# Products of turned probabilities and values issued for two key tiles at a time, with two more buffers for the turned tiles

## The chip, the cores and the metric

The kernel runs on one core of a Trainium2 chip. The metric is the device time of one execution in microseconds (us), lower is better.

## What is computed

The program is one forward pass of a small network on 1024 tokens of 1024 channels, in float32: a state-space layer, a layer with forgetting attention, then a block with a windowed attention over latents and 256 context tokens and a mixture of experts, and a block with a low-rank dense attention and a mixture of experts. What matters here are its three attentions. Cut to the essentials:

```python
# forgetting attention: 16 heads of 64, 1024 queries, causal
s = einsum('bhqd,bhkd->bhqk', qi, kt) + fqi[..., None] - fk[:, :, None, :]
p = softmax(where(kpos <= qpos, s, -inf)); o = einsum('bhqk,bhkd->bhqd', p, vt)
# windowed attention: 8 heads of 64 (2 of keys), blocks of 128 queries see 3 blocks of keys and 256 context keys
o = gqa_attend(qb, concat([kb, k_ctx]), concat([vb, v_ctx]), mask, sink_g, scale)
# dense attention: 8 heads with keys of 96 and values of 64, 1024 queries, 1280 keys
o = gqa_attend(qb, k_all, v_all, None, None, scale)
```

## The kernel before

Everything is cut into tiles of 128 tokens. An attention is a list of units (`run_units`, L1094). A unit makes the scores of some query tiles on TensorE into PSUM (tile `pA`), reduces their maximum on VectorE (L1019), takes the exponential on ScalarE (L1031) and so leaves probabilities with queries down the partitions. The products with the values need keys down the partitions, so `pv_steps` (L1035) has a step for each tile of 128 keys: for each of two streams `s` (two heads, or two groups of heads) it turns up to four probability tiles with transposes on TensorE into a PSUM tile `pT` (L1059, 3 buffers), copies that to a tile `pt` in SBUF (on ScalarE for stream 0, L1062; on VectorE for stream 1, L1064), and one step later multiplies it with the values (`av`, L1049):

```python
for s in range(2):
    nc.tensor.matmul(box["acc"][s * 64:(s + 1) * 64, c], lhsT=v(kt, s), rhs=pt[s][:, c],
                     start=(kt == 0), stop=(kt == last))
```

The values of a head are 64 wide. Stream 0 writes PSUM partitions 0 to 63 and stream 1 partitions 64 to 127, so the two use different halves of TensorE's columns. Such a float32 product is one instruction of the program and stands as two MATMUL records in the trace. The values' tile tells the attention: `vp` in the forgetting one, `vE` in the windowed one, `vpo` in the dense one.

A unit's products run beside the scores of the next unit (`merge`, L1077). The order in which the instructions of an engine finally stand is not the order of the code: a scheduler places them when the program is built, by what is ready, and each engine then executes its own list strictly in order. All buffers come from pools; an instruction that writes a buffer waits until its last reader is done. `finish` of the windowed attention (L1462) copies the accumulator out (`ots`), turns it back (L1459), scales it (`otE`) and stores it.

Behind the attentions runs other work: modulation rows on GpSimd (L361 to L367), whose sums go through TensorE (L385), and loads on the one hardware DMA queue that SyncE issues. After the dense attention come eight small products for the router (L1926) and the output projection (L241 to L243).

Of the kernel before, what the change touches and what calls it, by code (L numbers as in the profile page):

```python
# [20 lines left out]
P = 128  # L21
# [47 lines left out]
class Act:  # L69
    """Exact pairs hi + lo of an activation, [128, k, tokens] for each group of up to 512 tokens."""  # L70
# [13 lines left out]
    def span(self, k, m, cnt):  # L84
        """Token tiles m .. m + cnt of one group."""
        hi, lo = self.group(m // 4)
        c = slice(m % 4 * P, (m % 4 + cnt) * P)
        return hi[:, k, c], lo[:, k, c]


class ActK:
    """The same with one pair of tiles for each k; raw: buffers of values that are done with when those of
    channel tile k come."""
# [13 lines left out]
class Sink:  # L107
    """Takes the finished rows of a layer over while they are on chip: pairs of token tiles from a pool, and
    then(first tile, pair) for each."""
# [8 lines left out]
class Net:  # L118
# [17 lines left out]
    def tick(self):  # L136
        """Emits a few steps of the work that runs beside the main line: of the next thing in it (front) and
        of what is only needed later (behind, with a key and a weight for each step)."""
        for _ in range(self.rate[0]):
            if self.front:  # L140
                self.front.pop(0)()
        n = self.rate[1]
        while self.behind and self.behind[0][1] <= n:
            n -= self.behind[0][1]
            self.behind.pop(0)[2]()
# [44 lines left out]
    def col_source(self):  # L190
        """[128, 128] to load from, while the weights' buffers are free"""
# [5 lines left out]
    def columns(self, specs, name):  # L197
        """Vectors laid down the partitions: one transpose for up to 128 rows."""
# [15 lines left out]
    def rstd(self, ssq, n, width, name="rstd", bufs=2):  # L214
        """(ssq / width + eps) ** -0.5"""
# [7 lines left out]
    def load_w(self, W, c0, n):  # L223
        """Columns c0:c0+n of W as exact pairs hi + lo, one pair of tiles per 128 rows."""
        return [t for k in range(0, W.shape[0] // P, 2) for t in self.load_w2(W, k, c0, n)]

    def load_w2(self, W, k, c0, n):
        """Row tiles k and, if there is one, k + 1 of them."""
# [16 lines left out]
    def proj_tok(self, xT, W, c0, n, tiles, evict):  # L245
        """Rows are tokens: evict(first tile, count, psum[128, count, n])."""
# [14 lines left out]
    def proj_ch(self, xT, W, c0, n, evict):  # L261
        """Rows are output channels: evict(block of 128 channels, psum[128, 1024 tokens])."""
# [16 lines left out]
    def rms(self, tiles):  # L279
        """1 / rms of the rows of up to four tiles."""  # L280
# [7 lines left out]
    def norm_steps(self, pool, pair, gs, sh, hT, m0):  # L288
        """Steps for token tiles m0, m0 + 1 of hT: x * rstd * gs + sh; pair: x as [128, 2, 1024] (overwritten) or
        what gives it."""  # L290
# [28 lines left out]
    def to_T(self, pool, rows, kr, hT, m0, k, gs=None, sh=None):  # L319
        """Transposes columns kr*128.. of up to four [128 tokens, ...] tiles into channel tile k of hT, with an  # L320
        optional affine per channel."""
# [18 lines left out]

    def mod_steps(self, W, vecs, part, use):
        """Steps for one part of 1024 columns of the rows v @ W, with use(q, blocks, sel) called for each 128 of
        them: sel.T @ block is the row of a vector."""
# [33 lines left out]
    def mod_entry(self, out, q, blocks, sel, bias, gain):  # L377
        """Columns q.. of out [128, vectors, 8] from blocks[vector][i], sel.T @ block being 128 of its row: to
        it bias is added, or with a gain (1 + row + bias) * gain."""
# [12 lines left out]
    def mod_col(self, nv, bias, name, gain=None):  # L392
        """[128, vectors, 8]: the rows down the partitions; and what takes them."""
# [3 lines left out]
    def mod_row(self, nv, bias, name, gain=None):  # L397
        """The same as rows [1, vectors, 1024] in DRAM."""
# [19 lines left out]
    def start_a(self, pool, space, rows, W, hT):  # L418
        """Norm of x with the modulation of the first layer, into hT, and the first 256 columns of h @ W, channel
        tile by channel tile as the modulation comes in. Returns the first 512 columns of W, and the products as  # L420
        [chunk, group, step, channel]."""
# [24 lines left out]
        def fetch(k):  # L446
# [11 lines left out]
            else:  # L458
                # half of it in the buffers of the work behind, which so starts after this
# [24 lines left out]
        for k in range(KT):  # L484
# [16 lines left out]
            for m in range(NT):  # L501
                xh, xl = hT.span(k, m, 1)
                o = acc[m // 4][:, m % 4 // 2, m % 2 * 256:m % 2 * 256 + 256]
                for i, (x, y) in enumerate(((xh, w[k][0]), (xh, w[k][1]), (xl, w[k][0]))):
                    # two sums to a bank, which starts with the first of them
# [22 lines left out]
    def mods_2(self, layer):  # L528
        """Modulation of one layer of the second block for the latent and the context tokens: (1 + scale) g
        and shift of the first norm down the partitions, everything else as rows in DRAM."""  # L530
# [33 lines left out]

    def cmul(self, pool, outr, outi, xr, xi, yr, yi, shape, shared=False):
        """out = x * y (complex); shared: the imaginary part on GpSimd."""
# [17 lines left out]
    def s5_powers(self, keep, tp):  # L584
        """Small tables: abar^k, B scaled, C; the pairs of groups lie (half, state) down the partitions."""
# [50 lines left out]
        # descending powers for the way in, conjugates for the way out  # L636
# [3 lines left out]
        # coef = (abar - 1) / A  # L640
# [22 lines left out]
    def s5_in_tables(self, tp, ep, pin, bb):  # L663
        """Steps for E_d: abar^(7-j) B as [(j c), (half, state)]."""
# [20 lines left out]
    def s5_out_tables(self, tp, pw, bb):  # L685
        """Steps for G_d: conjugates of C abar^k for k = 1..8; M_d: Re(C abar^tau B) + D as block Toeplitz."""
# [3 lines left out]
        def start():  # L690
# [16 lines left out]
            # the halves of B side by side, zero elsewhere  # L707
# [4 lines left out]
        def step(q):  # L712
# [12 lines left out]
            # rows (pair, half, c') beside columns (tau, c)  # L725
# [16 lines left out]
    # The layers are generators: the following one, follow(pool, its context), takes the pool of the operands  # L742
    # of the last projection over, opens its own pools and yields the sink of that projection's rows; then it
    # goes on.

    def layer_a(self, x_d, follow):
        """x_d (DRAM) gets x + gate * S5(...)"""
# [11 lines left out]
        # x lies where its channel tiles will be  # L759
# [30 lines left out]
        # u, token tile j holds steps j of every chunk; transposed to [(j c), chunk]  # L790
# [62 lines left out]
        with ExitStack() as ctx:  # L853
            gp = self.pool("gA", 1, ctx=ctx)
            for nb in range(2):
                def evg(b, ps):
# [6 lines left out]
                    # from (step, chunk) to token order  # L863
# [14 lines left out]
    def resid_out(self, xT, W, segs, sink):  # L878
        """dst = src + gate * (xT.T @ W) for (gate, src, dst, tiles) over consecutive row tiles."""
# [31 lines left out]
    def s5_states(self, pool, U, S, nb):  # L911
        """b[chunk] = sum_j abar^(7-j) B u_j for the 16 groups of block nb, into S[:, :, :, 1:]."""
# [14 lines left out]
    def s5_scan_powers(self, tp, spw, pw):  # L927
        """spw[:, 0]: abar^(8 m) real part twice, spw[:, 1]: imaginary part negated and plain, m = 1..8.
        pw holds conjugates."""
# [9 lines left out]
    def s5_scan(self, pool, S, w):  # L939
        """S[n+1] <- abar^8 S[n] + S[n+1], in two levels of 8 x 16 chunks."""  # L940
# [27 lines left out]
    def s5_out(self, op, cb, U_d, S, y_d):  # L968
        """gelu(Re(C s) + D u) as [channel, (step, chunk)] of 128 channels, into y_d; returns it in SBUF. S: the
        states of this half, in DRAM for the first."""  # L970
# [14 lines left out]
        # even and odd groups sit on different PE rows and go to different banks  # L985
# [25 lines left out]

    def softmax_rows(self, pool, parts, p, rsum, scale=1.0, sink=None):
        """p <- exp(scale * S - max), rsum <- its row sums; returns minus the maximum.
        parts: (psum slice, slice of p) in order."""
# [8 lines left out]
        if sink is not None:  # L1023
            # sink holds minus the sink logit
# [10 lines left out]
    def pv_steps(self, pool, ps_, kts, v, done):  # L1035
        """Steps of the unnormalised P V of two streams of query tiles side by side:
# [1313 lines left out]
```

## Time and profile before

| | |
|---|---|
| runs shown | 4450.94, 4440.25 and 4452.07 us, median 4450.94 |
| profiled execution | span 4439.8 us, 0.4 us below the lowest run |
| TensorE busy | 4080.7 us, 92% of the span |
| VectorE, ScalarE, GpSimd busy | 62%, 45%, 39% |
| forgetting attention | about 1094 to 1397 us |
| windowed attention | about 1737 to 1934 us |
| dense attention | about 3298 to 3656 us |

A timeline row has the start, the time from the first start to the last end of a run of equal instructions, the engine, the source line, output and inputs, sizes and the count. The ends of matmuls are modelled and overlap the next one, so what an instruction costs TensorE is read as the distance from its start to the start of the next row.

### The profile page before, as it was taken

How to read it: one execution, taken by the hardware profiler on the slowest of the kernel's cores; microseconds unless marked ns; L12 is line 12 of the kernel's file. 1: busy time of each engine (PE TensorE's matmuls, PEld its weight loads, DVE VectorE, ACT ScalarE, POOL GpSimd, SP SyncE). 2: the span in 40 equal slices, each digit the busy share in tenths (PEclk: the TensorE clock that was granted, in tenths of full speed). 3: DMA queues.
4: the chain of work that ended last, by engine and by line, in shares of the span. 5: the costliest groups of instructions: out<-in, count | busy, mean ns of one | idle time of the engine just before them, and what ended most of it. 6: DMA issues, size and time to landing. Idle time of an engine off the chain costs nothing.

```text
span 4439.8 us, 58704 instructions
## 1 busy us (share of the span) xinstructions
PE 4080.7 (92%) x21145; PEld 2989.7 (67%) x21145; DVE 2764.4 (62%) x3988; ACT 1976.2 (45%) x3027; POOL 1743.5 (39%) x1965
## 2 busy tenths in 40 slices
PE   7878999998999999998799999979989999699996
PEld 6766777777556787567466666648865558588775
DVE  8866455451555636655776777763555544899887
ACT  4223333322543313432566666651344442477765
POOL 2888789997446786003111111136700000211100
PEclk9988999998999999998899999989999999799998
DMA  7546564445554543144588788763431015899996
GB/s 235 165 146 236 174 206 151 155 135 164 131 139 138 157 130 119 55 141 174 193 278 279 264 284 274 274 208 93 135 120 36 21 43 188 308 384 387 373 362 231
DMA packets 517542, 853.12 MB, mean 192 GB/s; under 512 B 68141, under 2 KB 304802, under 8 KB 516674
## 3 DMA queue, kind: packets, MB, share of 16 engines
q1 hardware_dynamic: 505298, 810.55, 53.5%
q0 software_dynamic: 11952, 38.82, 3.9%
q8 instruction: 167, 2.74, 0.2%
q14 instruction: 125, 1.02, 0.1%
HBM read 716.91 MB, written 132.31 MB: 191 GB/s over the span
## 4 chain that ended last, share of the span: by engine, by line
PE 64%; POOL 19%; DMA 6%; DVE 4%; issue 4%; ACT 2%; SPq 1%; POOLq 0%; ACTq 0%; DVEq 0%
PE pA L241 13%; PE pA L242 13%; PE pA L243 13%; PE pC L1049 7%; POOL mprod L361 6%; PE pC L2178 4%; PE pT L1059 4%; POOL mprod L362 4%; POOL S L959 2%; POOL scg L958 2%; POOL macc L365 2%; POOL macc L364 1%; POOL macc L367 1%; PE pT L2150 1%; POOL rstd L220 1%
## 5 line engine op out<-in xcount | busy, mean ns | idle before, releaser
L277 DVE TENSOR_TENSOR wlo<-fraw,whi 128x1024 fp32r<-128x1024 f32 x623 | 743.3, 1219 | 200.5 <-ACT whi L276 192.2
L276 ACT ACTIVATE whi<-fraw 128x1024 fp32r<-128x1024 f32 x623 | 650.2, 1059 | 274.3 <-PE pA L243 242.2
L241 PE MATMUL pA<-whi,ah 128*128 128x512 f32 (+3 forms) x1584 | 599.0, 379 | 19.1 <-DVE hkn L1132 6.3
L242 PE MATMUL pA<-wlo,ah 128*128 128x512 f32 (+3 forms) x1584 | 595.5, 376 | 5.4 <-DVE wlo L236 5.4
L243 PE MATMUL pA<-whi,al 128*128 128x512 f32 (+3 forms) x1584 | 593.3, 375 | 0.2 <-DVE al L277 0.2
L242 PE MATMUL pA<-wlo,xt 128*128 128x512 f32 x1024 | 412.3, 403 | 1.5 <-DVE wlo L277 0.8
L241 PE MATMUL pA<-whi,xt 128*128 128x512 f32 x1024 | 411.3, 403 | 0.0
L243 PE MATMUL pA<-whi,xt 128*128 128x512 f32 x1024 | 405.1, 396 | 0.0
L2191 POOL DMA_INDIRECT xs<-h_d,ixl x32 | 38.4, 1200 | 921.4 <-PE pT L2150 872.0
L361 POOL TENSOR_TENSOR mprod<-mraw,sil 128x512 f32<-128x512 f32 x320 | 359.7, 1124 | 62.3 <-DMA mraw<-mod_w 39.4
L362 POOL TENSOR_TENSOR mprod<-mprod 128x256 f32<-128x256 f32 x416 | 353.7, 850 | 30.5
L241 PEld LDWEIGHTS pA<-whi,ah 128*128 128x128 f32 x1584 | 306.6, 194 | 69.7 <-issue 10.3
L242 PEld LDWEIGHTS pA<-wlo,ah 128*128 128x128 f32 x1584 | 306.2, 193 | 57.2 <-DVE wlo L236 9.2
L243 PEld LDWEIGHTS pA<-whi,al 128*128 128x128 f32 x1584 | 306.2, 193 | 49.4 <-issue 0.7
L1019 DVE TENSOR_REDUCE st<-pA 128x1 f32<-128x640 f32 (+4 forms) x208 | 201.0, 967 | 184.7 <-PE pA L243 70.2
L235 ACT ACTIVATE whi<-wraw 128x1024 fp32r<-128x1024 f32 (+3 forms) x130 | 130.7, 1016 | 388.2 <-PE pA L243 187.1
L241 PEld LDWEIGHTS pA<-whi,xt 128*128 128x128 f32 x1024 | 192.5, 188 | 86.0 <-issue 40.6
L1923 POOL MEMSET rones<- 128x128 f32 x3 | 0.6, 205 | 616.8 <-PE pT L1059 420.0
L236 DVE TENSOR_TENSOR wlo<-wraw,whi 128x1024 fp32r<-128x1024 f32 (+3 forms) x130 | 171.0, 1332 | 115.1 <-ACT whi L235 112.3
L242 PEld LDWEIGHTS pA<-wlo,xt 128*128 128x128 f32 x1024 | 192.7, 188 | 73.3 <-issue 25.2
L241 PE MATMUL pA<-ah,whi 128*128 128x512 f32 x576 | 230.1, 403 | 6.6 <-ACT ah L276 3.7
L243 PE MATMUL pA<-ah,wlo 128*128 128x512 f32 x576 | 227.3, 397 | 3.8 <-DVE wlo L236 3.8
(575 smaller groups left out, 8938.6 us busy)
## 6 DMA issues: line engine op xcount, KB each, us to landing
fraw<-exp_w SPq DMA_DIRECT2D x632, 512.0 KB
wraw<-exp_w SPq DMA_DIRECT2D x132, 512.0 KB
mraw<-mod_w SPq DMA_DIRECT2D x192, 256.0 KB
mraw<-b_mod_w SPq DMA_DIRECT2D x48, 256.0 KB
wraw<-a_w_in SPq DMA_DIRECT2D x16, 512.0 KB
mraw<-kv_mod_w SPq DMA_DIRECT2D x32, 256.0 KB
wraw<-kv_w SPq DMA_DIRECT2D x16, 512.0 KB
kf_d<-hs SPq DMA_DIRECT2D x32, 256.0 KB
```

The source lines that it names most:

```text
L236: nc.vector.tensor_tensor(lo[:, :kk, :n], raw[:, :kk, :n], hi[:, :kk, :n].bitcast(F32), OP.subtract)
L241: mm(ps, lhsT=lh, rhs=rh, start=first, stop=False)
L242: mm(ps, lhsT=lh, rhs=rl, start=False, stop=False)
L243: mm(ps, lhsT=ll, rhs=rh, start=False, stop=last)
L276: self.nc.scalar.activation(hi, src, AF.Copy)
L277: self.nc.vector.tensor_tensor(lo, src, hi.bitcast(F32), OP.subtract)
L361: G(t, raw, v[:, 4 * h:4 * h + 4, None].to_broadcast([P, 4, P]), OP.mult)
L362: G(t[:, 0:2], t[:, 0:2], t[:, 2:4], OP.add)
L1019: nc.vector.tensor_reduce(st[:, i:i + 1], s, AX.X, OP.max, negate=True)
L1049: nc.tensor.matmul(box["acc"][s * 64:(s + 1) * 64, c], lhsT=v(kt, s), rhs=pt[s][:, c], start=(kt == 0), stop=(kt == last))
L1059: nc.tensor.transpose(pt[:, j * P:(j + 1) * P], ps_[s][j](kt), self.id)
L2178: nc.tensor.matmul(pc[t:t + 32], lhsT=xc[:, kk], rhs=raws[kk][:, n * 512:(n + 1) * 512], start=(k == 1), stop=(k == KT - 1))
```

## The change

`av` now takes several key tiles, and a step issues the products of the two tiles before it at every second tile, where it issued those of the last tile at each. The pool of turned tiles gets 8 buffers (7 in the dense attention) where it had 6 (5), and the windowed attention's `ots` and `otE` get one buffer where they had two. The diff also deletes comments and docstrings, leaving blank lines, which changes no instruction; lines after `av` stand one or two lower (L1049 becomes L1050, L1059 becomes L1060).

```diff
@@ pv_steps
-        def av(kt):
+        def av(*kts_):
             if not box:
                 box["acc"] = self.psC.tile([P, 512], F32, name="pC")
-            c, pt = parts.pop(kt)
-            for s in range(2):
-                nc.tensor.matmul(box["acc"][s * 64:(s + 1) * 64, c], lhsT=v(kt, s), rhs=pt[s][:, c],
-                                 start=(kt == 0), stop=(kt == last))
+            for kt in kts_:
+                c, pt = parts.pop(kt)
+                for s in range(2):
+                    nc.tensor.matmul(box["acc"][s * 64:(s + 1) * 64, c], lhsT=v(kt, s), rhs=pt[s][:, c],
+                                     start=(kt == 0), stop=(kt == last))
 
         def step(kt):
             j0 = min(j for j in range(nq) if kt < kts[j])
...
                 pt = self.psT.tile([P, 512], F32, name="pT")
                 for j in range(j0, nq):
                     nc.tensor.transpose(pt[:, j * P:(j + 1) * P], ps_[s][j](kt), self.id)
-                t = pool.tile([P, 512], F32, name="pt", bufs=6 if last < 9 else 5)
+                t = pool.tile([P, 512], F32, name="pt", bufs=8 if last < 9 else 7)
                 if s == 0:
                     nc.scalar.activation(t[:, c], pt[:, c], AF.Copy)
                 else:
                     nc.vector.tensor_copy(t[:, c], pt[:, c])
                 sb.append(t)
             parts[kt] = (c, sb)
-            if kt:
-                av(kt - 1)
+
+            if kt > 1 and kt % 2 == 0:
+                av(kt - 2, kt - 1)
 
         def end():
-            av(last)
+            av(*sorted(parts))
             done(box["acc"][:, :nq * P])
@@ window_units, finish
-            ot = ap_.tile([P, 512], F32, name="ots", bufs=2)
+            ot = ap_.tile([P, 512], F32, name="ots", bufs=1)
             nc.scalar.activation(ot, acc, AF.Copy)
-            op = ap_.tile([P, 2, 4, HD], F32, name="otE", bufs=2)
+            op = ap_.tile([P, 2, 4, HD], F32, name="otE", bufs=1)
```

The multiset of TensorE's instructions is the same before and after; the scheduler puts them in another order. Three places of TensorE's list show how. In its rows a product is `MATMUL pC<-pt,...`, with `x2` when the products of both streams stand side by side; a transpose is `pT<-cst,...` with the probabilities' tile (`whi`, `wlo`, `pO`, `pE`) last.

The first place is in the forgetting attention, in one of the units on the queries' second half. Before:

```order
L1059 MATMUL pT<-cst,wlo 128x128 x4
L1049 MATMUL pC<-pt,vp 64x512 x2
L1059 MATMUL pT<-cst,whi 128x128 x4
L1329 MATMUL pA<-khh,q_10006 128x512
L1330 MATMUL pA<-kll,qe_8910 128x512
```

and the same place of the change:

```order
L1060 MATMUL pT<-cst,wlo 128x128 x4
L1050 MATMUL pC<-pt,vp 64x512
L1060 MATMUL pT<-cst,whi 128x128 x4
L1050 MATMUL pC<-pt,vp 64x512
L1331 MATMUL pA<-khh,q_10006 128x512
L1332 MATMUL pA<-kll,qe_8910 128x512
```

The two products that stood side by side now stand apart, with four transposes of the next key tile between them.

The second place is the last unit of the dense attention, where no scores are left to run beside. Before:

```order
L1059 MATMUL pT<-cst,whi 128x128
L1049 MATMUL pC<-pt,vpo 64x512 x2
L1059 MATMUL pT<-cst,wlo 128x128 x2
L1059 MATMUL pT<-cst,pO 128x128 x2
L1059 MATMUL pT<-cst,whi 128x128 x2
```

and of the change:

```order
L1060 MATMUL pT<-cst,whi 128x128
L1050 MATMUL pC<-pt,vpo 64x512
L1060 MATMUL pT<-cst,wlo 128x128 x2
L1060 MATMUL pT<-cst,pO 128x128 x2
L1050 MATMUL pC<-pt,vpo 64x512
L1060 MATMUL pT<-cst,whi 128x128 x2
```

Here too one pair of products is taken apart by four transposes.

The third place is in the windowed attention, where the queries of the next unit are turned (`qdE`). Before, and then of the change:

```order
L1425 MATMUL pT<-cst,qdE 128x128 x4
L1049 MATMUL pC<-pt,vE 64x512
L1425 MATMUL pT<-cst,qdE 128x128 x4
L1049 MATMUL pC<-pt,vE 64x512
L1059 MATMUL pT<-cst,pE 128x128 x4
```

```order
L1427 MATMUL pT<-cst,qdE 128x128 x8
L1050 MATMUL pC<-pt,vE 64x512 x2
L1060 MATMUL pT<-cst,pE 128x128 x4
```

Here two products that stood apart now stand side by side.

## Rows read from the trace of the kernel before

**Rows 1.** Page, busy time by engine over the whole span:

```profile
PE 4080.7 (92%) x21145; PEld 2989.7 (67%) x21145; DVE 2764.4 (62%) x3988; ACT 1976.2 (45%) x3027; POOL 1743.5 (39%) x1965
```

**Rows 2.** Busy time by stretch: the three attentions, and two stretches after the first:

```profile
core 0: us, PE busy (x) PEld busy (x) DVE busy (x) ACT busy (x) POOL busy (x), PEclk, DMA share, GB/s
1094.00:1397.00 303.00, 300.63 (x1773) 174.70 (x1773) 169.84 (x265) 149.92 (x357) 146.20 (x208) 0.98 0.50 124
1737.00:1934.00 197.00, 185.37 (x1028) 107.44 (x1026) 121.69 (x262) 102.88 (x246) 10.72 (x16) 0.99 0.19 60
3298.00:3656.00 358.00, 355.06 (x1696) 196.66 (x1695) 193.43 (x413) 164.67 (x351) 0.20 (x1) 1.00 0.09 27
...
1397.00:1465.00 68.00, 63.39 (x276) 52.51 (x277) 38.52 (x42) 16.51 (x28) 36.10 (x44) 0.92 0.63 198
1465.00:1535.00 70.00, 64.84 (x327) 53.64 (x325) 55.07 (x76) 33.19 (x58) 64.82 (x75) 1.00 0.44 139
```

**Rows 3.** Products with the values, one source line: records by values' tile:

```profile
L1049 PE MATMUL pC<-pt,vp x384: 272/564/1116, 1106.6 to 1396.6; 128*64 128x512 f32 x96, 128*64 128x384 f32 x32, 128*64 128x256 f32 x32, 128*64 128x128 f32 x32
...
L1049 PE MATMUL pC<-pt,vpo x320: 592/593/644, 3301.0 to 3655.1; 128*64 128x512 f32 x160
...
L1049 PE MATMUL pC<-pt,vE x168: 592/593/644, 1746.9 to 1933.0; 128*64 128x512 f32 x168
```

**Rows 4.** Timeline of TensorE in the forgetting attention:

```profile
1129.93 0.61 PE L1059 MATMUL pT<-cst,whi 128*128 128x128 f32 x4
1130.38 0.60 PE L1059 MATMUL pT<-cst,wlo 128*128 128x128 f32 x4
1130.90 1.08 PE L1049 MATMUL pC<-pt,vp 128*64 128x512 f32 x4
1131.91 0.66 PE L1059 MATMUL pT<-cst,whi 128*128 128x128 f32 x4
...
1156.81 0.65 PE L1049 MATMUL pC<-pt,vp 128*64 128x256 f32 x4
1157.40 0.61 PE L385 MATMUL pT<-ones,macc 128*128 128x1 f32 x4
...
1159.16 0.44 PE L1049 MATMUL pC<-pt,vp 128*64 128x128 f32 x4
1159.53 0.66 PE L1059 MATMUL pT<-cst,wlo 128*128 128x128 f32 x4
```

**Rows 5.** Timeline of TensorE in the dense attention, and a run of three products in the windowed one:

```profile
3607.50 1.07 PE L1049 MATMUL pC<-pt,vpo 128*64 128x512 f32 x2
3608.50 0.44 PE L1059 MATMUL pT<-cst,wlo 128*128 128x128 f32 x2
...
1921.82 1.93 PE L1049 MATMUL pC<-pt,vE 128*64 128x512 f32 x6
1923.68 0.38 PE L1449 MATMUL pA<-khE,q2E 128*128 128x256 f32 x1
```

**Rows 6.** Waits of TensorE in the forgetting attention, then in the windowed one:

```profile
PE pT L1059 <- DMA zp<-zf_d: 0.6, 1, 0.6
PE pA L1329 <- ACT wlo L1031: 0.4, 1, 0.4
...
PE pA L1443 <- ACT pE L1031: 7.4, 11, 2.2
...
PE pT L1059 <- ACT pt L1062: 0.3, 1, 0.3
```

**Rows 7.** Waits of GpSimd from 1090 to 1397 us:

```profile
POOL macc L367 <- PE pT L385: 111.0, 13, 23.4
```

**Rows 8.** Timeline of TensorE after the dense attention, and the same router products after the windowed one:

```profile
3657.55 3.09 PE L1926 MATMUL pC<-rw,rones 128*128 128x16 f32 x16 [0.89 <-DVE rw L1921]
3664.97 0.79 PE L241 MATMUL pA<-whi,ah 128*128 128x512 f32 x1 [4.33 <-ACT ah L276]
...
1948.30 1.85 PE L1926 MATMUL pC<-rw,rones 128*128 128x16 f32 x16
```

## The prediction

> **What bounds the kernel now.** Over the whole span TensorE is busy 92% of the time, more than any other engine [rows 1]. The change touches only the three attentions, so I read the busy time by stretch next: TensorE is busy 300.6 of 303 us in the forgetting attention, 185.4 of 197 in the windowed one and 355.1 of 358 in the dense one, while VectorE and ScalarE are at 46% to 62% there. The granted clock is 0.98 to 1.00, the upper of its levels [rows 2]. In these stretches TensorE is the limit, and the waits say the same: in the steady part of the forgetting attention it waited 0.6 us for a load and 0.4 us for an exponential. In the windowed one the largest wait is for an exponential (7.4 us in 11 pieces), and the wait of a transpose for a copy into a turned tile is 0.3 us [rows 6]. So a wait for turned tiles, which more buffers could shorten, hardly exists. What counts is how long TensorE's own list is, and the change reorders this list.
>
> **What a product costs, by its neighbour.** The timeline gives the price. In the dense attention one product of 512 queries (two records) starts at 3607.50 and what follows it at 3608.50: 1.00 us [rows 5]. In the forgetting attention the products of both streams side by side (four records) start at 1130.90 and the next transpose at 1131.91: 1.01 us for two [rows 4]. The two halves of the columns work at the same time if, and only if, the two products stand next to each other in TensorE's list. A product that stands alone leaves half the array idle and costs as much as a pair. So I count not products but blocks of adjacent ones. By the same reading a block of 256 queries costs 0.59 us and one of 128 costs 0.37 [rows 4]; a step of 128 is thus about 0.21, and one of 384 lies at 0.80.
>
> **The change, attention by attention.** There are 192, 84 and 160 products (records halved, [rows 3]), the same before and after. I went through TensorE's whole list of before and of the changed program and counted blocks.
>
> Forgetting attention: before, 68 blocks of 512 queries (28 of them pairs), 22 of 384, 16 of 256 and 23 of 128, and one run of a 256 pair and a 128 pair. After, 80 of 512 (16 pairs), 20 of 384, 29 of 256 (10 paired, nine of these with a product of 128 of the other stream) and 15 of 128, and the same one run. The difference is 12 x 1.01 - 2 x 0.80 + 13 x 0.59 - 8 x 0.37 = 12.1 - 1.6 + 7.7 - 3.0 = +15.2 us. Each block also has an entry: four transposes followed by transposes take 0.45 us (1129.93 to 1130.38), followed by products 0.52 (1130.38 to 1130.90) [rows 4], so an entry costs about 0.1 us, and 15 more blocks 1 to 2 us, of which I take 2 since a product now also goes in where a transpose had led straight into scores. Together +17 us, in a stretch with 1 us of waits to hide it. This is the first place shown with the change, in unit after unit.
>
> Windowed attention: 65 blocks before, 63 after. Pairs are gained where the next queries are turned (the third place shown) and lost in runs of transposes. That is -2 us. One buffer for `ots` and `otE` costs nothing: each is used once a unit, ten units in 197 us, so the buffer is free some 20 us before it is wanted; without that cover a unit would wait for one store.
>
> Dense attention: 141 blocks before, 144 after (the second place shown): +3.0 us and 0.3 for entries. The eight router products also move. Before, they ran at 3657.55 in a gap in which the next projection waited until 3664.97 for its input anyway [rows 8]; after, they stand some 29 instructions inside that projection, where the list is dense. In such a place the same sixteen records took 1.85 us [rows 8]. So +5 us here.
>
> The extra buffers give at most what TensorE waits for copies, under 1 us where the waits name them [rows 6]; I take nothing. ScalarE and VectorE do the same copies as before and have over a third of their time free. Distances in the list from a transpose to the product that needs its copy stay as long or grow, so I expect no new wait; if the order makes some, they are like those of the windowed attention, 7.4 us in all, and they make it slower.
>
> Sum: +17 - 2 + 5 = **+20 us**. Against the profiled execution, 4439.8 us, this is 4460. The runs shown have a median 11 us above it, so for a median I add the 20 us to 4450.94 and predict **4470 us**, 0.45% slower. A change of less than about 0.3%, 13 us, can't be told from none.
>
> **Rivals.** *The delay is absorbed later (same).* After the forgetting attention TensorE is idle for 4.6 us of 68 and 5.2 us of 70 [rows 2]. If what it waits for there comes from loads and GpSimd work that don't move with it, up to 9.8 us are given back: 20 - 10 = +10, 4461 us. Against it: GpSimd stood 111 us in the attention waiting for TensorE to take its sums [rows 7], so it can't run ahead and moves along. It decides if more than 7 us come back.
>
> *The chip profits as the code reads (faster).* If the four products of two key tiles stood together, a run of three products in the windowed attention prices it: 1.86 us for a pair and a single [rows 5], so a pair and a pair about 1.9. The dense attention would take 40 x 1.9 = 76 us where 141 blocks take 142, the windowed one 21 x 1.9 = 40 where it takes 66, the forgetting one perhaps 75 where its blocks sum to 105: -122 us, 4329 us. The Trainium skill, TensorEngine Tiling (Array Packing), Tiling Modes, says under Key Properties that changing the tiling mode drains TensorE, which speaks for fewer and longer runs of such products; by that rule halving the visits is right, and the rows above show the cost of an entry as about 0.1 us, no more. Against this rival stands the list itself: blocks don't become fewer but go from 336 to 352, and TensorE executes its list in order. To come out faster by 0.3% some 33 us would have to be found beyond my sum; all waits of TensorE in the three stretches, idle time by the rows 2.4 + 11.6 + 2.9 = 17 us, don't reach it [rows 2].
>
> *More is lost (slower still).* If the later exponentials in the windowed attention double its waits, 7.4 us more [rows 6], and the entries cost twice what I took, it is +30, 4481 us.
>
> **How the numbers follow.** My forecast, +14 to +35 us, gets 0.76: the prices are read from rows, and the order is known. Absorbed, within 13 us either way, 0.19. The faster rival and all else that is faster, 0.05. So faster 0.05, same 0.19, slower 0.76. The range reaches from 4450, the absorbed case on a median that may itself lie some us lower since one of three runs is at 4440.25, to 4486, +35 on the median.
>
> **What the profile after would show.** Single products with `x2` in the timeline and fewer `x4` in the forgetting attention, this stretch 17 us longer with TensorE still busy nearly all of it; the dense one longer by 3 to 5, the windowed one shorter by about 2; everything between shifted and otherwise alike. I am wrong if a lone product costs less than 1.00 us beside its new neighbours, if the stretch after the forgetting attention is shorter by what that one has grown, or if waits on copies (L1062, L1064) turn out to have been hidden in the durations I took as prices.

## The result, and the profile after

The changed kernel is slower. Four timed runs have a median of 4473.26 us (4467.21 to 4475.15) beside 4449.5 us (4440.25 to 4452.07) for the kernel before, +23.8 us. The ratio is 1.006 with a 95% interval of 1.0048 to 1.0072. The profiled execution has a span of 4465.4 us, 25.7 more than before's. (Differences of spans and stretches are taken before rounding.) The page's line of busy times:

```profile
PE 4095.7 (92%) x21145; PEld 2989.8 (67%) x21145; DVE 2770.5 (62%) x3988; ACT 1975.5 (44%) x3027; POOL 1746.5 (39%) x1965
```

TensorE has the same 21145 records and is busy 15.0 us longer than in [rows 1]; VectorE has the next largest difference, 6.1 us. Over the whole span this alone says little: in a second trace of before, taken later, TensorE is busy 4067.0 us, 13.7 less than in the first. The busy times by stretch, for the three attentions and the two stretches behind the first (columns as in [rows 2]):

```profile
1090.00:1411.00 321.00, 316.39 (x1773) 177.60 (x1773) 171.10 (x264) 148.87 (x357) 148.30 (x210) 0.98 0.48 118
...
1753.00:1949.00 196.00, 181.66 (x1029) 106.57 (x1030) 120.48 (x262) 103.54 (x248) 11.02 (x17) 1.00 0.18 62
...
3314.00:3675.00 361.00, 358.39 (x1697) 197.31 (x1695) 193.58 (x412) 164.78 (x351) 0.20 (x1) 1.00 0.09 27
...
1411.00:1479.00 68.00, 62.40 (x274) 51.24 (x274) 37.88 (x40) 16.27 (x26) 38.05 (x45) 0.95 0.62 199
1479.00:1549.00 70.00, 65.70 (x326) 54.98 (x324) 57.62 (x76) 35.01 (x60) 64.98 (x73) 0.98 0.41 133
```

The windows are laid so that TensorE's count agrees with [rows 2] to within two records. The same 1773 records of the forgetting attention now take 321 us where they took 303. The windowed attention's window is 1 us shorter and the dense one's 3 us longer. The two stretches behind the forgetting attention are as long as before and as full, so nothing is given back there. The timeline of TensorE in one of its units shows what the 18 us consist of:

```profile
1210.90 1.07 PE L1050 MATMUL pC<-pt,vp 128*64 128x512 f32 x2
1211.91 0.65 PE L1060 MATMUL pT<-cst,wlo 128*128 128x128 f32 x4
1212.49 1.07 PE L1050 MATMUL pC<-pt,vp 128*64 128x512 f32 x2
1213.49 0.66 PE L1060 MATMUL pT<-cst,whi 128*128 128x128 f32 x4
```

Two products of one stream each (`x2`) with four transposes between them: 1.01 and 1.00 us from the start of each to the next row, where [rows 4] has both streams in one block (`x4`) for 1.01 us. No wait that could make up the 18 us has come in. The waits of TensorE in the forgetting attention, first the largest one of before, then the list of after:

```profile
PE pT L1059 <- ACT p L1344: 11.1, 3, 10.7
...
PE pT L1060 <- ACT p L1346: 12.7, 3, 12.3
PE pC L1050 <- DVE rs L1377: 0.6, 1, 0.6
PE pT L1060 <- DMA zp<-zf_d: 0.6, 1, 0.6
PE pA L1331 <- ACT wlo L1031: 0.4, 1, 0.4
```

and in the windowed one:

```profile
PE pA L1445 <- ACT pE L1031: 9.5, 9, 2.8
PE pT L1461 <- ACT ots L1466: 4.6, 8, 0.8
```

Apart from 0.6 us for `rs` they are those of before, within some 2 us. The largest, for the first probabilities `p`, stands at the attention's begin, ahead of the steady part that the prediction reads. Its longest piece is 10.7 us before and 12.3 after, but 11.5 and 11.1 in a second trace of each, so this difference can be chance. (The wait for `ots` is 3.7 us in the trace of before and 3.8 in the second trace of after, so a cost of its single buffer doesn't show.) The end of the dense attention, and the router products in the projection behind it:

```profile
3661.84 1.07 PE L1050 MATMUL pC<-pt,vpo 128*64 128x512 f32 x2
3662.84 0.44 PE L1060 MATMUL pT<-cst,wlo 128*128 128x128 f32 x2
3663.12 0.38 PE L1060 MATMUL pT<-cst,pO 128*128 128x128 f32 x2
3663.43 1.07 PE L1050 MATMUL pC<-pt,vpo 128*64 128x512 f32 x2
3664.43 0.44 PE L1060 MATMUL pT<-cst,whi 128*128 128x128 f32 x2
...
3692.31 1.85 PE L1928 MATMUL pC<-rw,rones 128*128 128x16 f32 x16
3694.01 0.48 PE L243 MATMUL pA<-whi,al 128*128 128x512 f32 x1
```

The last unit shows the pattern again, and the router products cost 1.70 us (3692.31 to 3694.01) between the projection's.

To follow the time from end to end I laid the traces side by side by TensorE's projection products, whose order is the same in all of them. An attention's length is from the start of the last such product ahead of it to the start of the first behind it (the dense one from a fixed product at its begin). In us, with the second trace of each kernel that the experiments gave:

| | before | before, 2nd | after | after, 2nd |
|---|---|---|---|---|
| up to the forgetting attention | 1081.2 | 1076.6 | 1077.7 | 1081.7 |
| forgetting attention | 317.0 | 314.9 | 334.9 | 337.8 |
| between | 326.2 | 326.5 | 328.0 | 329.8 |
| windowed attention | 207.3 | 208.0 | 205.5 | 208.7 |
| between | 1368.2 | 1367.4 | 1369.8 | 1368.6 |
| dense attention | 365.1 | 365.4 | 368.3 | 368.6 |
| behind | 774.8 | 779.2 | 781.1 | 781.0 |
| span | 4439.8 | 4437.9 | 4465.4 | 4476.0 |

The same program differs by up to 5 us in the stretches outside the attentions and by some 3 within one. The forgetting attention's +18.0 to +22.8 and the dense one's +2.9 to +3.5 (each trace of after against each of before) stand out from that. Part of the scatter in the forgetting attention goes with TensorE's clock: of the two traces of a kernel the longer one has the lower granted clock there, 0.96 beside 0.98 before and 0.95 beside 0.97 after.

### The profile page after: what moved, and what is told of

Its sections match the earlier page's. It is cut to its first block, busy times and chain, and to the rows that moved or that the text cites. A ratio compares the mean times of both kernels' runs of the same rounds, so it can differ in the third digit from the quotient of the medians.

```text
span 4465.4 us, 58707 instructions
## 1 busy us (share of the span) xinstructions
PE 4095.7 (92%) x21145; PEld 2989.8 (67%) x21145; DVE 2770.5 (62%) x3988; ACT 1975.5 (44%) x3027; POOL 1746.5 (39%) x1965
## 4 chain that ended last, share of the span: by engine, by line
PE 67%; POOL 17%; DMA 6%; DVE 5%; issue 4%; ACT 2%; SPq 1%; POOLq 0%; ACTq 0%; DVEq 0%
PE pA L241 14%; PE pA L242 14%; PE pA L243 13%; PE pC L1050 7%; POOL mprod L361 5%; PE pC L2180 4%; PE pT L1060 4%; POOL mprod L362 3%; POOL S L959 2%; POOL scg L958 2%; POOL macc L365 1%; POOL macc L367 1%; PE pT L2152 1%; POOL macc L364 1%; PE pA L1331 1%
## 5 line engine op out<-in xcount | busy, mean ns | idle before, releaser
L242 PEld LDWEIGHTS pA<-wlo,xt 128*128 128x128 f32 x1024 | 192.9, 188 | 73.2 <-issue 25.2
L242 PE MATMUL pA<-al,whi 128*128 128x512 f32 x576 | 229.0, 398 | 1.1 <-DVE al L277 1.0
```

Of the source, the lines that this page charges most:

```text
L242: mm(ps, lhsT=lh, rhs=rl, start=False, stop=False)
```

## The experiments

The theory to test, that of the blocks: TensorE is the limit, the time follows the number of blocks of adjacent products in its list, and a product that stands alone costs as much as a pair because only adjacent products use both halves of the columns. Its rivals: the buffers make the difference; the price of a lone product hides a wait for its copy; the loss lies outside the attentions. Ratios are to the kernel before on the same chip. Where an experiment adds lines, its line numbers are a few higher than those of before.

**The two parts of the change, one at a time.** The buffers alone:

```diff
-                t = pool.tile([P, 512], F32, name="pt", bufs=6 if last < 9 else 5)
+                t = pool.tile([P, 512], F32, name="pt", bufs=8 if last < 9 else 7)
...
-            ot = ap_.tile([P, 512], F32, name="ots", bufs=2)
+            ot = ap_.tile([P, 512], F32, name="ots", bufs=1)
```

(and `otE` likewise).

> The kernel before with the buffers of the change alone: 8 (7) for turned tiles, one for `ots` and `otE`; products still issued for one key tile at a time. TensorE's list has the same blocks of products as before (130, 65 and 141). Theory of the blocks (time follows the number of blocks of adjacent products in TensorE's list): no change, within 3 us of before. Theory of the buffers (the other part of the change makes the difference, by turned tiles that lie longer or by units that wait for `ots`): most of the +24 us is seen here.

Measured 4446.29 us beside 4440.21, ratio 1.0009 (1.0000 to 1.0018). This is 3 us more than I gave it, at the edge of what can be told from nothing. Its trace has none of it in the attentions (316.2, 208.5 and 365.1 us). Two tiles at a time with the old buffers, so the diff of the change without the lines above:

> The change without its buffers: products issued for two key tiles at a time, with 6 (5) buffers for turned tiles and two for `ots` and `otE`. TensorE's list has the same blocks as in the change (145, 63, 144). Theory of the blocks: +15 to +25 us, about as the change. Theory of the buffers: under +8 us; or, if two tiles at a time need the buffers, clearly more than +25 us through waits for turned tiles.

Measured 4462.86 us beside 4440.21, ratio 1.0047 (1.0034 to 1.0061), +22.6 us; attentions 334.8, 207.9 and 367.7 us. So the issue for two tiles carries the loss, and the buffers none of the attentions' part of it. The change with its buffers, but two tiles at a time in the forgetting attention alone:

```diff
-            if kt > 1 and kt % 2 == 0:
-                av(kt - 2, kt - 1)
+            if last in (3, 7):
+                if kt > 1 and kt % 2 == 0:
+                    av(kt - 2, kt - 1)
+            elif kt:
+                av(kt - 1)
```

> Two key tiles at a time in the forgetting attention alone, the buffers as in the change; the windowed and the dense attention one tile at a time. Blocks 145, 64 and 141 in place of 130, 65 and 141. Theory of the blocks: +17 us in the forgetting attention and about 0 elsewhere, so +15 to +20 us in all. If the rest of the change (the router products and the dense attention) carries most of it, under +12 us.

Measured 4466.19 us beside 4441.41, ratio 1.0046 (1.0034 to 1.0058), +24.8 us by the medians and +20.4 by the ratio: above the +15 to +20 I gave it. The trace has the forgetting attention 14.6 us longer, the windowed one 1.4 and the dense one as before (365.2). So the forgetting attention carries the largest part, but of the 26.1 us that this trace is longer in all, 10.0 lie outside the attentions, and the blocks don't explain them.

**All products side by side.** One key tile at a time, old buffers; each product also depends on the other stream's copy, so that the scheduler finds both ready together. What is computed stays the same.

```diff
             for s in range(2):
-                nc.tensor.matmul(box["acc"][s * 64:(s + 1) * 64, c], lhsT=v(kt, s), rhs=pt[s][:, c],
-                                 start=(kt == 0), stop=(kt == last))
+                i = nc.tensor.matmul(box["acc"][s * 64:(s + 1) * 64, c], lhsT=v(kt, s), rhs=pt[s][:, c],
+                                     start=(kt == 0), stop=(kt == last))
+                self.tc.add_manual_dep(i.ins, cps[1 - s].ins.name, BOTH, reason="side by side")
```

> The kernel before, one key tile at a time and the old buffers, but each product also depends on the other stream's copy, so that both products of a key tile become ready together. In TensorE's list all products then stand side by side: 95, 40 and 79 blocks in place of 130, 65 and 141. Theory of the blocks, by the prices of the prediction (1.0, 0.8, 0.6 and 0.37 us a block by size, 0.1 us an entry): 219 us in place of 346, so -127 us if TensorE stays the limit and nothing new is waited for, -90 to -127 with some new waits. If a lone product is not as dear as a pair (the price hides waits for the copies), the gain is under 40 us.

Measured 4349.8 us beside 4440.21, ratio 0.9793 (0.9779 to 0.9806), -90.4 us. That is far from the 40 us of the hidden wait and at the near end of what I gave the blocks. The dense attention, by stretch:

```profile
3275.00:3572.00 297.00, 287.16 (x1699) 185.08 (x1698) 191.21 (x416) 161.19 (x352) 0.20 (x1) 1.00 0.10 31
```

About the same records as in [rows 2] in 297 us where they took 358: 62 blocks fewer, 61 us less. The forgetting attention is where the rest of the forecast stayed away: 312.8 us, only 4 less than before. That is taken up below.

**All products apart.** The opposite: TensorE's order within a unit is fixed so that each product stands behind one stream's transposes of the next tile.

```diff
             for s in range(2):
                 pt = self.psT.tile([P, 512], F32, name="pT")
                 for j in range(j0, nq):
-                    nc.tensor.transpose(pt[:, j * P:(j + 1) * P], ps_[s][j](kt), self.id)
+                    queued(nc.tensor.transpose(pt[:, j * P:(j + 1) * P], ps_[s][j](kt), self.id))
+                if kt:
+                    av(kt - 1, s)
```

(`queued` puts an instruction behind the last one given to it, in order of issue alone; `av` issues one stream's product.)

> The opposite: the two products of a key tile are kept apart, one behind the turning of stream 0 of the next tile, one behind that of stream 1. 187, 75 and 158 blocks in place of 130, 65 and 141; buffers as before. Theory of the blocks: 427 us in place of 346, so +81 us (+65 to +95). If a lone product is not as dear as a pair, under +30 us.

Measured 4534.11 us beside 4440.21, ratio 1.0212 (1.0198 to 1.0226), +93.9 us. A lone product is dear wherever it stands:

```profile
1165.30 0.61 PE L1066 MATMUL pT<-cst,whi 128*128 128x128 f32 x4
1165.83 1.07 PE L1056 MATMUL pC<-pt,vp 128*64 128x512 f32 x2
1166.84 0.66 PE L1066 MATMUL pT<-cst,wlo 128*128 128x128 f32 x4
1167.42 1.07 PE L1056 MATMUL pC<-pt,vp 128*64 128x512 f32 x2
1168.43 0.50 PE L1336 MATMUL pA<-khh,q 128*128 128x512 f32 x1
```

1.01 us each. Here the four transposes ahead of a product take 0.53 us (1165.30 to 1165.83), or 0.58 (1166.84 to 1167.42) when a product stands ahead of them as well, against 0.45 among transposes [rows 4].

**Is it the column halves?** As with all side by side, but both streams' products go to stream 0's half:

```diff
+                h = 0 if 0 < kt < last else s
-                i = nc.tensor.matmul(box["acc"][s * 64:(s + 1) * 64, c], lhsT=v(kt, s), rhs=pt[s][:, c],
+                i = nc.tensor.matmul(box["acc"][h * 64:(h + 1) * 64, c], lhsT=v(kt, s), rhs=pt[s][:, c],
                                      start=(kt == 0), stop=(kt == last))
```

> As the run with all products side by side (95, 40 and 79 blocks, -90 us), but for all key tiles of a unit save the first and the last both streams' products are added to stream 0's half of the columns; this adds the two streams up, so it changes what is computed there. Nothing else in TensorE's list moves. If a pair costs what a single costs because the two halves of the columns work at the same time, these pairs now cost double: 359 us of blocks in place of 219, so +140 us on the pairs, about +50 us against before (+30 to +60). If a pair is cheap because its second product saves the entry or a wait, it stays at -90 us.

Measured 4447.43 us beside 4441.41, ratio 1.0013 (1.0005 to 1.0022): +6 us against before, some 96 above the run with the halves, each taken against its own before. The expectation, +30 to +60, was too high for two reasons. It added 140 us, a whole further block for each such pair; at the 0.85 us that the rows below show it is 119. And the forgetting attention lost only 22 us against the run with the halves where some 45 of the 119 were counted, since that run was waiting there already (below). The price itself stands in the timeline, first a pair in different halves (the first tile of a unit), then one in the same half:

```profile
1163.13 1.08 PE L1052 MATMUL pC<-pt,vp 128*64 128x512 f32 x4
1164.14 0.50 PE L1335 MATMUL pA<-khh,q 128*128 128x512 f32 x1
...
1165.93 1.93 PE L1052 MATMUL pC<-pt,vp 128*64 128x512 f32 x4
1167.79 0.66 PE L1063 MATMUL pT<-cst,whi 128*128 128x128 f32 x4
```

1.01 us and 1.86 us for the same four records side by side. Adjacency alone gives 0.15 us (2.01 for two lone ones, 1.86 for two in one half); the other 0.85 us come from the two halves working at the same time. (The second product then also adds to the same rows of PSUM as the first; this run doesn't separate that from the shared columns.) The Trainium skill, TensorEngine Tiling (Array Packing), Tiling Modes, says under Key Properties that different tiles of the array can load weights and multiply in parallel; these rows agree as to the products, and add that they do so here only when they follow each other in the list.

**Two tiles at a time, side by side.** The change as it is, with each product also behind the other stream's copy (the lines as above, inside the loop over `kts_`):

> The change as it is (two key tiles at a time, 8 (7) buffers, one for `ots` and `otE`), with each product also behind the other stream's copy of its tile. Blocks 95, 40 and 79, the same as in the run with one tile at a time and the products side by side, which took 4349.8 us, -90 us. Theory of the blocks: the same -90 us within 6 us, so that two tiles at a time by themselves neither cost nor give anything once the products stand side by side. If two tiles at a time cost by themselves, about -70 us; if the additional time between turning and product, and the buffers, save waits, -100 us or better.

Measured 4331.36 us beside 4441.41, ratio 0.9749 (0.9736 to 0.9761), -110 us, so the third case: 20 better than one tile at a time with the same blocks. The attentions are 288.6, 184.5 and 304.1 us, those of one tile at a time 312.8, 182.1 and 304.2: the difference lies in the forgetting attention. Two runs cross the two parts. One tile at a time with the change's buffers:

> One key tile at a time with the products side by side, as the run at -90 us, and the buffers of the change: 8 (7) for turned tiles, one for `ots` and `otE`. TensorE's list is the same; SyncE's differs in a few places. The run with two tiles at a time, these buffers and the same blocks took -110 us, 20 less, nearly all of it in the forgetting attention. If the buffers give these 20 us, now that products wait for both copies: -105 to -112 us. If two tiles at a time give them: -88 to -94 us.

Measured 4346.38 us beside 4442.58, ratio 0.9779 (0.9765 to 0.9793), -96.2 us, between the two cases and nearer to the second; forgetting attention 308.8 us. And two tiles at a time with 6 (5) buffers:

> Two key tiles at a time with the products side by side, as the run at -110 us, but 6 (5) buffers for turned tiles as before the change (one for `ots` and `otE`, as there). TensorE's list is the same. If the buffers give the 20 us between the two runs with side by side products: -88 to -95 us. If two tiles at a time (which change when the loads of the next queries are issued) give them: -105 to -112 us.

Measured 4330.52 us beside 4442.58, ratio 0.9753 (0.9740 to 0.9767), -112 us; forgetting attention 286.8 us. So it is the issue for two tiles; of the buffers nothing clear shows. The waits say what it does; their sizes are those of two single executions, of 4359.63 us with one tile at a time and 4319.74 with two, which lie further apart than the medians, so they are at the upper end. Of TensorE in the forgetting attention, two of the rows with one tile at a time (with 8 buffers):

```profile
PE pA L1334 <- DMA q<-qf_d: 4.8, 5, 1.8
PE pA L1335 <- DMA qe<-qf_d: 4.6, 5, 2.1
```

With two tiles at a time these two rows are missing from the list, with 6 buffers as with 8 (with the four products together, below, 2.9 us of them are back). Once the pairs make TensorE faster, the loads of the next unit's queries come too late, 9.4 us in 10 pieces. Behind most of these waits the clock is lower. By stretch, with one tile at a time around the first of them, then with two over all these units:

```profile
1160.00:1185.00 25.00, 25.00 (x164) 15.38 (x162) 15.82 (x24) 13.75 (x35) 15.20 (x22) 1.00 0.53 124
1185.00:1192.00 7.00, 4.03 (x25) 2.62 (x23) 1.84 (x5) 2.70 (x9) 0.00 (x0) 0.90 1.09 224
1192.00:1206.00 14.00, 14.00 (x85) 9.50 (x84) 7.57 (x12) 4.34 (x9) 9.35 (x13) 0.80 0.53 117
1206.00:1220.00 14.00, 14.00 (x100) 8.96 (x98) 9.59 (x16) 8.54 (x22) 7.87 (x12) 1.00 0.32 77
```

```profile
1176.00:1350.00 174.00, 174.00 (x1198) 110.42 (x1196) 112.45 (x177) 95.51 (x232) 98.14 (x140) 1.00 0.61 146
```

After the idle time of 1185 to 1192 the granted clock, an average of the two levels, is 0.80 for 14 us, in which 85 records are done where 100 are done at 1.00. The ten pieces are five pairs, one for each next load of `q` and `qe`; the clock falls to its lower level behind four of them and not behind the third, 1.0 us in all. Over the attention, TensorE is busy 282.4 us of 309 with one tile at a time and 271.4 of 287 with two: of the 22 us, 11 are idle time and 11 the slower work. The times at the lower level behind the four waits add up to 20.5 us; at half the clock that is an estimate of 10 us lost, so the clock accounts for nearly all of the slower work. Why the loads are issued in time with two tiles at a time was not settled; the order of SyncE's queue differs in several places.

**The four products of two tiles together.** Each product depends on all four copies:

```diff
+            two = [(kt, *parts.pop(kt)) for kt in kts_]
+            for kt, c, pt, _ in two:
...
+                    for _, _, other, cps in two:
+                        for x, cp in zip(other, cps):
+                            if x is not pt[s]:
+                                self.tc.add_manual_dep(i.ins, cp.ins.name, BOTH, reason="side by side")
```

> What the change reads like: the four products of two key tiles stand together, each behind all four copies. 48, 23 and 40 blocks, nearly all of four products. Theory of the blocks: a four is worth two pairs less one entry of 0.1 us, so 209 us in place of 219 for the pairs: -100 us against before, 10 better than pairs. If waiting for four copies stops TensorE, worse than the pairs (-90 us). The rival of the prediction, that the change profits as its code reads, priced this at -122 us.

Measured 4317.96 us beside 4441.41, ratio 0.9720 (0.9705 to 0.9736), -123.5 us. It beats both kernels and is the fastest run here. In the dense attention:

```profile
3405.86 1.94 PE L1051 MATMUL pC<-pt,vpo 128*64 128x512 f32 x8
3407.73 0.44 PE L1065 MATMUL pT<-cst,wlo 128*128 128x128 f32 x2
```

Two pairs together take 1.87 us, where two pairs apart take 2 x 1.01. Its attentions are 284.5, 179.5 and 303.1 us: 2 to 5 us better than pairs in the first two, only 1 in the third, where 40 fours should have given 6. There, against the pairs with two tiles at a time, TensorE's busy time does fall, from 285.6 to 278.6 us, but its idle time grows from 18.6 to 24.5: what joining the pairs gives in this attention is waited away.

**The same two kernels once more**, for their traces (the table above):

> The kernel before once more, for its trace alone: it tells how much of a distance between two traces at one place is chance. The trace after has two places outside the attentions where it loses against the trace before without new order in TensorE's list: about 3.7 us at the router's logits before the last experts, where the granted clock is lower, and 3.9 us in the last 60 us. Theory of chance: this trace of the same program has one of the two steps also, or differs from the first one by 3 us and more at another place outside the attentions. Theory that they are the change's: both places as in the first trace of before, within 1 us. In the attentions both theories expect the first trace's lengths within 2 us.

> The changed kernel once more, for its trace alone. Theory of chance for the two places outside the attentions: at least one of the two steps (3.7 us at the router's logits, 3.9 us in the last 60 us) is gone. Theory that they are the change's: both are there again. Both expect the forgetting attention 15 to 18 us longer than before and the dense one 3 to 5 us longer.

4439.71 and 4477.77 us, one run each, beside 4442.58. The first place is chance. The last 24 records of the router's logits, in the first trace of before, its second and the trace of after, and the clock around them in the two of before:

```profile
3778.59 3.10 PE L1956 MATMUL pC<-rw,h2t 128*128 128x16 f32 x24
```

```profile
3773.88 5.14 PE L1958 MATMUL pC<-rw,h2t 128*128 128x16 f32 x24
```

```profile
3800.65 5.14 PE L1958 MATMUL pC<-rw,h2t 128*128 128x16 f32 x24
```

```profile
3776.00:3783.00 7.00, 5.69 (x43) 5.58 (x41) 1.94 (x5) 1.39 (x6) 7.00 (x5) 0.74 1.03 417
```

```profile
3771.00:3779.00 8.00, 8.00 (x39) 7.91 (x38) 1.20 (x2) 0.60 (x1) 8.00 (x5) 0.50 1.02 417
```

The same program does them in 3.10 or in 5.14 us, the latter with the clock at the lower level throughout. Over this place the second trace of before has 3.7 us more than the first, as after has; the second trace of after has the same 3.7, in neighbouring rows. From the last projection product ahead of the logits to the first transpose behind them, all 14 traces taken here show one of two times, whichever kernel it is: 50.9 us in six of them (the first trace of before is one) and 54.6 in eight. The second place, 3.9 us at the last products, is in both traces of after and in neither of before; it is also in the trace with the buffers alone and not in the one with two tiles and the old buffers, so it goes with the buffers. But it is given back at once: from one product some 60 us ahead of the end, the same in each, to the end of the span it is 59.6 and 59.6 us before and 59.9 and 58.7 after. My expectation that one of the two places would be gone in the second trace of after was wrong, and so was the one of 15 to 18 us for its forgetting attention, which is 20.8 us longer than in the first trace of before.

**The blocks' account.** With the prediction's prices (1.01, 0.80, 0.59 and 0.37 us a block by size) and no entries, against the lengths measured in the traces, each as the difference to before (130, 65 and 141 blocks). For products that follow in the same half, the second counts 0.85 us by the 1.86 us above, and accordingly for smaller sizes:

| | blocks | by the prices | measured |
|---|---|---|---|
| after | 145, 63, 144 | +15.2, -2.0, +3.0 | +18.0, -1.9, +3.2 |
| all apart | 187, 75, 158 | +46.6, +10.1, +17.2 | +53.7, +10.8, +20.1 |
| side by side, same half | 95, 40, 79 | +16.9, -5.7, -8.2 | +17.8, -3.7, -9.7 |
| side by side, one tile | 95, 40, 79 | -28.6, -24.4, -62.6 | -4.1, -25.2, -60.9 |
| side by side, two tiles | 95, 40, 79 | -28.6, -24.4, -62.6 | -28.3, -22.9, -61.0 |
| four together | 48, 23, 40 | -33.4, -27.1, -68.9 | -32.4, -27.9, -62.0 |

Seventeen of eighteen numbers agree within some 7 us, most within 3. The eighteenth is the forgetting attention that waits for its loads. The kernels with longer lists fit without any term for waits; of those with shorter lists the one whose query loads came late needs one, and the four products together in the dense attention, 7 us off, gained 6 us of idle time.

## Why the prediction was right

**The bound and the price.** That TensorE's own list is the limit, and that a lone product costs a pair, are shown from both sides: 84 blocks more by count (336 to 420) gave +94 us, 122 fewer gave -90 to -112. The step that most could have failed, a price read off two rows, holds because the halves work at the same time: 1.01 us for a pair in both halves against 1.86 in one.

**The forgetting attention, forecast +17.** Measured +18.0 in the profiled execution, 14.6 to 20.8 over the four traces that have the same blocks there, against the first trace of before. Of the 18.0, 16.0 us are busy time of TensorE and 2.0 idle time, 1.6 of it the longer wait at the begin, which can be chance. The 15.2 us of blocks are the core of it. The 2 us of entries are of the size of what such traces differ by, so that term alone is not shown here, and its price was rounded up: the two rows give 0.07 us, not 0.1. In the run with all apart, 57 blocks more leave 7.1 us over the prices, some 0.12 us a block, near the estimated 0.1.

**The windowed attention, forecast -2:** -1.9 in the first trace, +1.3 in the second, so it can't be told from nothing. **The dense one, forecast +5:** +3.2 in the attention (against 3.3 for blocks and entries) and 1.7 for the router products, +4.9.

**The buffers, forecast nothing.** Right for the attentions. Alone they measured +6 us with an interval from 0 to 8; the trace puts it outside the attentions (6.0 us there, 3.7 of them at the logits), where single stretches of the same program differ by up to 5 us. Whether anything of it is real stays open.

**The sum.** In the profiled execution the forecast terms come to 18.0 - 1.9 + 3.2 + 1.7 = +21.0 us against +20. The other 4.7 us of the span's 25.7 are not in the sum: -3.5 ahead of the first attention and +3.7 at the logits, both chance by the second trace of before; +1.9 and +1.7 between the attentions; and +0.9 left over in the rest. The between stretches were not followed further. Outside the attentions the four traces with the change's blocks in the forgetting attention are 6 to 11 us longer than the two of before (3550 us); all traces here lie between 3543 and 3563 us there, so whether the change costs something outside beyond the router products stays open. That the total comes so close, +20 against +23.8 by the medians, is in part luck, since these terms could have come out larger.

**The rivals.** The delay was not absorbed: the stretch behind the forgetting attention is 1.9 us longer, not shorter, and GpSimd's wait for TensorE to take its sums grew from 111.0 us [rows 7] to 120.6 in the same stretch of after, so it did move along, as argued. The faster rival failed as the prediction said, on the list. Its price was right, though: the four products of two tiles, once they really stand together, gave -123.5 us where it was priced at -122, and took 1.87 us where 1.9 was estimated; by attention it had priced -30, -26 and -66 us, and -32.4, -27.9 and -62.0 were measured. The halved number of entries is the smaller part of that: of the 123.5 us, 110 to 112 come from pairs with two tiles at a time, and the rest from joining two pairs. The rule on draining in the Trainium skill, TensorEngine Tiling (Array Packing), Tiling Modes, Key Properties, agrees in sign. Here joining two pairs is worth 0.15 us; whether a drain is what it saves, no run shows.

## What to carry to other kernels

Where two products use different halves of TensorE's columns, count how often they really stand next to each other in its final list; a scheduler that takes whatever is ready first can set them apart when their inputs come from different engines, as ScalarE's and VectorE's copies here. Making both wait for both inputs gave 2 to 2.5%, while issuing more of them at once in the code, without that, set more of them apart (why the scheduler did so was not followed). After such a gain, look again for what is late next: here it was the loads of the next queries, and with them the clock.

## What was not expected of the hardware

The slower work behind short waits cost about as much as the waits themselves: 11 us of idle time, most of it for the query loads in pieces of 0.5 to 2.1 us, came with 11 us more of busy time, with the granted clock lower behind four of the five loads (0.80 for 14 us behind the one shown). And the same small products of one program take 3.10 or 5.14 us by the level of the clock; the place around them takes 50.9 or 54.6 us, nothing between, in 14 traces of 12 kernels. Two single traces can differ by these 3.7 us without any cause in the kernel.
